# Streaming encoder, two layers: a shared pool of PSUM banks, a later place for layer 1's constants, other places for the norm sums

## The chip, the cores and the metric

One core of a Trainium2 chip runs the whole program. The metric is the device time of one execution in microseconds (us), the median of three runs. The engines are TensorE (PE; its weight loads are PEld), VectorE (DVE), ScalarE (ACT) and GpSimd (POOL); SyncE (SP) issues the transfers.

## What is computed

A two-layer encoder for 512 frames of one new stream and 16 frames of each of 8 running streams, all in fp32, model width 1024. Each layer is

```
h    = rmsnorm(x) @ w_in            # u_a, g_a, u_b, q, k, v
a    = rglru(conv4(u_a)) * gelu(g_a)             # gated linear recurrence, 256 wide
b    = s5(u_b); z = gelu(b + d*u_b); b = z*sigmoid(z @ w_glu)   # complex diagonal recurrence
c    = attention(rope(q), rope(k), v)            # 8 query heads, 2 kv heads, chunks of 64,
                                                 # window 128, one sink per head
x    = x + concat(a, b, c) @ w_out
x    = x + square(relu(rmsnorm(x) @ w_up)) @ w_down           # 1024 -> 4096 -> 1024
```

and one rmsnorm stands at the end. Outputs are y for both kinds of stream and the new states (convolution tail, recurrence states, rotated keys and values).

## The kernel before

Columns are frames, rows are features. The frames are split into two groups `g` of 320 (256 of the new stream, 64 of four running streams), kept in `xT` for the whole run. A product of 128 output rows and 320 frames is a `Unit`: its weights (two halves of 4 tiles) are loaded by SP, split by ACT (`wh`, L243) and DVE (`wl`, L244) into two fp32r parts, and multiplied in three passes (L274 to L276), 12 matmuls for each half of the contraction, 24 for a unit and a group. The very first projection (layer 0, group 0) is done in plain fp32 instead, 4 matmuls a half (L271; the profile shows two rows for each).

`stream(items)` (L278) turns a list of units and plain calls into a generator that yields after each half. A unit takes one of three "mm" banks of PSUM; its evacuation is called in the middle of the next unit, by `clear()` (L285), and put off as long as the unit's norm has no factor `r` yet. `Norm` (L332) squares the rows as they come, `flush()` sums them by ones-matmuls (L374), `finish()` takes the reciprocal root on DVE (L387 to L401) and spreads it by three matmuls (L411) and an ACT copy (L413), with high priority.

Three mixers run beside the projections and the MLP: `lru` (gates L759), `s5` (transposes L176, input products L822, scan L837 to L845, output products L855 and L858, gate L886) and `attention` (`own` L916, `sprobs` L948, `probs` L983, `turned` L999, `sturned` L957, `values` L1012, `svalues` L965; softmax in `soft`, L924 to L946). They are generators too; `TURNS` (L1055) writes their order by hand, `weave` (L322) mixes their steps with halves of the surrounding stream.

PE executes in the written order (L1158). On the other engines a planner orders the instructions when the kernel is built: by its own estimate of when each is ready, the earlier in the program first, high priority ahead of all. A pool slot (a bank, a buffer) is given to a tile when an earlier one is released.

PSUM has eight banks, split by tag: 3 "mm", 2 "att" (attention, the gates of lru, the turn of v in group 0), 2 "s5", 1 "fin" (norm sums). `sprobs` and `probs` take two banks each and hold them until the last exponential (L936) has read them. `own` takes one, released by the copy L922.

`layer_small` (L614) and `s5_const` (L528) prepare a layer's small matrices: four complex products (`cmul`, L545 to L548; for layer 1 all on POOL), transposes of the result (L553), four more products for C (L561 to L564), the product M (L570), then the tables of cosine and sine by doubling (L584 to L605). They use the one table `tab`, which layer 0's s5 reads until its last scan. For layer 1 they are called at the last MLP chunk of layer 0's first group (L1210 to L1213).

The MLP runs in four chunks of 8 `up` and 8 `down` units (`mlp`, L1102), chunks 1 and 2 with both groups per unit. `up_evac` (L1095) is DVE L1097, ACT L1098, POOL copy L156 (called in L1099), DVE L1100; its tile `t` has two buffers.

Of the kernel before, what the change touches and what calls it, by code (L numbers as in the profile page):

```python
# [19 lines left out]
NG = 320  # L20
# [127 lines left out]
def encoder_kernel(ctx: ExitStack, tc: tile.TileContext, a, o):  # L148
# [16 lines left out]
    pm = pool("pm", 1, space=bass.MemoryType.PSUM)  # L165
    banks = {"mm": 3, "att": 2, "s5": 2, "fin": 1}

# [89 lines left out]
    class Unit:  # L257


        def __init__(self, src, prods, norm=None, full=False, raws=None):  # L260
            self.src, self.prods, self.norm, self.full, self.raws = src, prods, norm, full, raws
            self.w = None

# [14 lines left out]
    def stream(items):  # L278


        items = list(items)
        units = [i for i in items if isinstance(i, Unit)]
        wait, late = [], []

        def clear(all_=False):  # L285
            for f in late:
                f()
            late.clear()
            while wait and (wait[0][0].norm is None or wait[0][0].norm.r is not None):
                unit, evac, pt = wait.pop(0)  # L290
                more = evac(pt)
                if more is not None:
                    late.append(more)

        for it in items:
            if not isinstance(it, Unit):
                it()
                continue
            it.load()
            n = units.index(it) + 1  # L300
            if n < len(units):
                units[n].load()
            for m, evac in it.prods:
                m = m() if callable(m) else m
                pt = bank("mm")[:, 0:NG]
                for half in range(2):
                    it.half(pt, m, half)
                    if half == 0:
                        clear()
                    yield  # L310
                wait.append((it, evac, pt))
            it.w = None
        clear()
        clear()
        assert not wait
# [212 lines left out]
    def s5_const(L, K):  # L528
# [21 lines left out]
        for q in range(2):  # L550
            b = bank3("s5", 4, 128)
            for i in range(4):
                transpose(b[:, i], Rp[:, 4 * q + i].rearrange("p r s c -> p (r s c)"))  # L553
            act(K["B"][:, 4 * q:4 * q + 4], b, AF.Copy)
# [12 lines left out]
        yield  # L567
        b = bank("s5")[:, 0:256].rearrange("p (k r c) -> p k r c", k=8, r=2)
        for k in range(8):
# [76 lines left out]
    def in_evac(L, P, g, q, kind, i, pt):  # L646
# [17 lines left out]
        elif kind == "ub":  # L664
            tt(q.ub[:, i], pt, r, OP.mult)
        elif kind == "ga":
            t = tp.tile([128, NG], F32, tag="t", name="t", bufs=2)
            tt(t, pt, r, OP.mult)
            gelu2(V, q.ga[:, i], t)
        elif kind == "v":  # L670
            vT = tp.tile([128, NG], F32, tag="t", name="t", bufs=2)
            tt(vT, pt, r, OP.mult)
            gcopy(q.vS, vT[:, 256:320])

            def turn():
                b = bank3("mm" if g else "att", 2, 128)
                for j in range(2):
                    transpose(b[:, j], vT[:, 128 * j:128 * j + 128])
                act(kvs[L]["vt"][:, 2 * g:2 * g + 2], b, AF.Copy)
                dma(o["vs"][L, g], q.vS)  # L680
                if g == 1:
                    dma(o["vp"][L], kvs[L]["vt"][:, 3])

            return turn
        else:
            sw = tp.tile([128, NG], F32, tag="sw", name="sw", bufs=2)
            for p in range(0, 128, 64):
                act(sw[p:p + 32], pt[p + 32:p + 64], AF.Copy)
                act(sw[p + 32:p + 64], pt[p:p + 32], AF.Copy)  # L689
            G.tensor_tensor(sw, sw, q.sinr, OP.mult)  # L690
            if kind == "q":
                t = tp.tile([128, NG], F32, tag="t", name="t", bufs=2)
                tt(t, pt, q.cosr, OP.mult)
                tt(q.q[:, i], t[:, 0:256], sw[:, 0:256], OP.add)
                v4 = lambda z: z[:, 256:320].rearrange("p (b t) -> p b t", t=16)
                tt(q.qS[:, :, i], v4(t), v4(sw), OP.add)
            else:
                t = tp.tile([128, NG], F32, tag="t", name="t", bufs=2)
                tt(t, pt, q.cosr, OP.mult)  # L699
# [8 lines left out]
    def in_proj(L, g, norm, q, raws=None):  # L708
# [11 lines left out]
        def factors():  # L720
# [5 lines left out]
            for t in (q.cosr, q.sinr):  # L726
                G.tensor_tensor(t, t, q.r, OP.mult)

        evac = lambda kind, i: lambda pt: in_evac(L, None, g, q, kind, i, pt)
        items = [Unit(w_in[n], [(lambda: norm.h, evac(kind, i))], norm, norm.full, raws if n == 0 else None)  # L730
                 for n, (kind, i) in enumerate(units)]
        return [begin, items[0], norm.flush, items[1], factors] + items[2:]


    def lru(L, P, g, q, mix, c):
# [15 lines left out]
        for ct in range(2):  # L751
# [5 lines left out]
            for n, dst in enumerate((t_, i_)):  # L757
                b = bank("att")[:, 0:LP]
                mm(b, lhsT=P["bd"][n][:, ct], rhs=xc, start=True, stop=True)  # L759
# [31 lines left out]
    def s5(L, P, g, q, mix, c):  # L791
# [9 lines left out]
        for ct, gs in cts:  # L801
            if ct:
                yield
            u2 = c.at(640 * ct, 8, 4, 16, parts=80)
            b = bank3("s5", 4, 128)[0:80]
            for t in range(4):
                transpose(b[:, t], u[:, ct, t::4])
            act(u2.rearrange("p g t c -> p t g c"), b.rearrange("p t (g c) -> p t g c", c=16), AF.Copy)
        for ct, gs in cts:
            yield  # L810
            u2 = c.at(640 * ct, 4, 128, parts=80)
            b = bank3("s5", 4, 80)
            for k in range(4):
                transpose(b[:, k], u2[:, k])
            V.tensor_copy(Us[:, ct], b)
        for ct, gs in cts:
            yield
            d, jz = D[:, gs], J[:, gs]
            bs = [bank3("s5", 4, 80) for r in range(2)]
            for k in range(4):  # L820
# [26 lines left out]
        for ct, gs in cts:  # L847
            yield
            d = D[:, gs]
            y2 = c.at(1280 + 640 * ct, 4, 4, 32, parts=80)  # L850
            bs = [bank3("s5", 4, 64)[0:80] for r in range(2)]
            tc2 = lambda t: t.rearrange("p t c -> p (t c)")
# [8 lines left out]
        for ct, gs in cts:  # L861
            y2 = c.at(1280 + 640 * ct, 4, 4, 32, parts=80)
            yield
            b = bank3("s5", 4, 80)
            for t in range(4):
# [17 lines left out]
        for ct in range(2):  # L883
            b = bank("s5")[:, 0:NG]
            for k in range(2):
# [10 lines left out]
    def attention(L, P, g, q, mix, c, cs):  # L896
# [19 lines left out]
        def own():  # L916
            b = bank3("att", 4, 128)[0:16]
            for hf in range(2):
# [29 lines left out]
        def sprobs():  # L948
            bs = [bank3("att", 2, 256) for hf in range(2)]
            for hf, b in enumerate(bs):  # L950
# [6 lines left out]
        def sturned(hf):  # L957
            b = bank3("att", 4, 128)
            for n in range(2):
# [5 lines left out]
        def svalues(hf):  # L965
            b = bank3("att", 2, 64)
            for n in range(2):
# [15 lines left out]
        def probs(cq):  # L983
# [3 lines left out]
            if cq < 2:  # L987
                for pe in pes:
                    G.memset(pe[:, :, 0:64], 0.0)
                    G.memset(pe[:, :, 256:320], 0.0)  # L990
            bs = [bank3("att", 2, 256) for kv in range(2)]
            for pr in range(2):
# [6 lines left out]
        def turned(cq, kv):  # L999
            j, kts, nk, k0, st, w0 = geo(cq)  # L1000
            b = bank("att").rearrange("p (t n q) -> p t n q", t=2, n=2)
            for kt in kts:
# [9 lines left out]
        def values(cq):  # L1012
            j, kts, nk, k0, st, w0 = geo(cq)
            b = bank("att")[:, 0:256]
            for kv in range(2):
# [72 lines left out]
    def out_proj(L, g, mix, hm):  # L1088
# [4 lines left out]
        return [begin] + [Unit(a["w_out"][L, k], [(lambda: mix["mix"](0), evac(k))]) for k in range(8)]  # L1093

    def up_evac(norm, am, f, pt):  # L1095
        t = tp.tile([128, NG], F32, tag="t", name="t", bufs=2)
        V.scalar_tensor_tensor(t, pt, 0.0, norm.r, OP.max, OP.mult)  # L1097
        act(t, t, AF.Square)  # L1098
        gcopy(am[:, f, 0], t)  # L1099
        tt(am[:, f, 1], t, am[:, f, 0].bitcast(F32), OP.subtract)  # L1100

    def mlp(L, c, gs, hm, nxt=None, norms=None, fresh=()):  # L1102
# [17 lines left out]

        ups = [Unit(a["w_up"][L, 8 * c + f], [up(g, f) for g in gs], hm[gs[0]] if fresh and f < 2 else None) for f in range(8)]
        items = [begin] + ups + [Unit(a["w_down"][L, c, k], [down(g, k) for g in gs]) for k in range(8)]
        for g in fresh:
            items[2:2] = [lambda g=g: hm[g].flush()]
            items[4:4] = [lambda g=g: hm[g].finish()]
        return items
# [53 lines left out]
    for L in range(DEPTH):  # L1180
# [15 lines left out]
        run(stream(mlp(L, 0, (1,), hm, fresh=(1,))))  # L1196
        run(stream(mlp(L, 1, (0, 1), hm)))
        run(stream(mlp(L, 2, (0, 1), hm)))
        nxt = (lambda g: Norm(g, None)) if last else (lambda g: Norm(g, n1(L + 1)))
        norms = {}  # L1200
        F = stream(mlp(L, 3, (0,), hm, nxt, norms))
        if last:
            run(F)
            end = [norms[0].flush, lambda: finals(0)]
            items = mlp(L, 3, (1,), hm, nxt, norms)
            items[3:3] = end[:1]
            items[5:5] = end[1:]
            run(stream(items))
        else:
            P = {}  # L1210
            small = layer_small(L + 1, P)
            next(small)
            weave(small, 2, F, 24)  # L1213
            run(F)
# [36 lines left out]
```

## Time and profile before

| | |
|---|---|
| median of 3 runs | 1453.31 us (1453.0 to 1453.5) |
| the profiled execution | 1452.91 us, of which its span in the trace 1451.1 |
| TensorE | 1374.8 us busy (95%), mean granted clock 0.968 |
| VectorE, ScalarE, POOL | 882.4 (61%), 651.5 (45%), 360.0 us (25%) |
| DMA | 156.24 MB, mean 108 GB/s |

In a timeline a row is: start and duration in us, engine, line, operation, output tile <- input tiles, shape, count; in brackets the idle time of the engine ahead of it and what ended it. In the waits, "A <- B: total, times, longest" is idle time of A that B's end ended. "PEclk" is the granted TensorE clock as a share of full speed. Times of a matmul row overlap with the next row's.

### The profile page before, as it was taken

To read this page: it belongs to the slowest core of one execution; us is meant where nothing else is said; L and a number is where in the kernel's file an instruction comes from. 1 tells how busy PE (TensorE), PEld (TensorE's weight loads), DVE (VectorE), ACT (ScalarE), POOL (GpSimd) and SP (SyncE) were. 2 spreads that over 40 slices of the span, in tenths; PEclk is the share of its full clock that TensorE was granted. 3 is DMA by queue.
4 is the path that set the end of the run, shared out by engine and by line. 5 is a ranking of instruction groups with operands and counts; after the bars stand their busy time and mean duration, and the time that the engine had idled before them with its cause. 6 is when DMAs were issued, how large, how long until landed. Compare 5 with 4: busy or idle time off the path is not lost.

```text
span 1451.1 us, 25432 instructions
## 1 busy us (share of the span) xinstructions
PE 1374.8 (95%) x9444; PEld 1313.1 (90%) x9444; DVE 882.4 (61%) x1726; ACT 651.5 (45%) x1347; POOL 360.0 (25%) x581
## 2 busy tenths in 40 slices
PE   7867979999999999999989998899999999999997
PEld 5656869899999999999978998899999999999997
DVE  7785698756644344357787768775664434434674
ACT  4354765545433123134675668553543312313543
POOL 5654277601001001008343224320100100100111
PEclk9978989999999999999999999999999999999998
DMA  6211332344422222233423342333443222223452
GB/s 244 83 55 50 107 104 86 105 154 141 151 95 75 79 79 75 73 110 119 155 90 104 123 128 82 112 96 130 146 145 102 73 73 78 76 80 104 152 175 94
DMA packets 91387, 156.24 MB, mean 108 GB/s; under 512 B 14336, under 2 KB 18304, under 8 KB 91264
## 3 DMA queue, kind: packets, MB, share of 16 engines
q1 hardware_dynamic: 91264, 154.63, 31.9%
q8 instruction: 74, 1.21, 0.3%
q14 instruction: 49, 0.40, 0.1%
HBM read 151.02 MB, written 3.37 MB: 106 GB/s over the span
## 4 chain that ended last, share of the span: by engine, by line
PE 84%; DVE 7%; POOL 3%; ACT 2%; issue 2%; DMA 2%; SPq 0%; DVEq 0%; ACTq 0%; POOLq 0%
PE mm L274 26%; PE mm L275 25%; PE mm L276 25%; PE att L176 1%; PE att L1017 1%; PE s L858 1%; PE att L996 1%; PE fin L411 1%; PE s L886 1%; PE att L971 1%; PE s L822 1%; DVE wl L244 1%; DMA raw<-w_in 1%; PE s L176 0%; PE fin L374 0%
## 5 line engine op out<-in xcount | busy, mean ns | idle before, releaser
L274 PE MATMUL mm<-bigr,wh 128*128 128x320 f32 x2592 | 820.1, 316 | 1.6 <-POOL bigr L156 1.6
L276 PE MATMUL mm<-bigr,wl 128*128 128x320 f32 x2592 | 806.1, 311 | 1.1 <-DVE wl L244 1.1
L275 PE MATMUL mm<-bigr,wh 128*128 128x320 f32 x2592 | 806.5, 311 | 0.3 <-DVE bigr L1100 0.3
L243 ACT ACTIVATE wh<-raw 128x512 fp32r<-128x512 f32 x520 | 327.4, 631 | 508.5 <-PE mm L275 479.4
L274 PEld LDWEIGHTS mm<-bigr,wh 128*128 128x128 f32 x2592 | 492.1, 190 | 15.5 <-issue 8.8
L275 PEld LDWEIGHTS mm<-bigr,wh 128*128 128x128 f32 x2592 | 492.5, 190 | 1.5 <-DVE bigr L1100 0.6
L276 PEld LDWEIGHTS mm<-bigr,wl 128*128 128x128 f32 x2592 | 491.9, 190 | 1.4 <-DVE wl L244 1.4
L244 DVE TENSOR_TENSOR wl<-raw,wh 128x512 fp32r<-128x512 f32 x520 | 377.0, 726 | 190.1 <-ACT wh L243 179.7
L156 POOL TENSOR_SCALAR bigr<-t 128x320 fp32r<-128x320 f32 x128 | 61.0, 478 | 648.5 <-ACT t L1098 648.5
L1084 DVE TENSOR_TENSOR xT<-xT,mm 128x320 f32<-128x320 f32 x160 | 77.7, 486 | 130.4 <-PE mm L276 130.3
L1097 DVE SCALAR_TENSOR_TENSOR t<-mm,r 128x320 f32<-128x320 f32 x128 | 62.3, 489 | 87.9 <-PE mm L276 87.3
L1098 ACT ACTIVATE t<-t 128x320 f32<-128x320 f32 x128 | 60.1, 472 | 114.0 <-DVE t L1097 107.9
L1100 DVE TENSOR_TENSOR bigr<-t,bigr 128x320 fp32r<-128x320 f32 x128 | 65.4, 511 | 68.9 <-POOL bigr L156 68.7
L368 POOL TENSOR_TENSOR ss<-ss,sq 128x320 f32<-128x320 f32 x58 | 55.1, 950 | 185.3 <-ACT sq L361 180.9
L361 ACT ACTIVATE sq<-xT 128x320 f32<-128x320 f32 x66 | 30.5, 462 | 21.5 <-POOL ss L368 14.1
L348 ACT ACTIVATE bigr<-xT,sm 128x320 fp32r<-128x320 f32 x56 | 30.6, 560 | 14.7 <-DVE xT L1084 13.6
L690 POOL TENSOR_TENSOR sw<-sw,cs 128x320 f32<-128x320 f32 x20 | 17.9, 897 | 68.2 <-ACT sw L689 54.4
L996 PE MATMUL att<-kT,q 64*64 64x192 f32 (+2 forms) x256 | 16.6, 347 | 19.1 <-ACT att L936 19.1
L271 PE MATMUL mm<-bigf,raw 128*128 128x320 f32 x104 | 32.2, 456 | 2.5 <-DVE t L699 2.5
L349 DVE SCALAR_TENSOR_TENSOR bigr<-xT,sm,bigr 128x320 fp32r<-128x320 f32 x56 | 34.0, 611 | 0.7 <-ACT bigr L348 0.4
L996 PEld LDWEIGHTS att<-kT,q 64*64 64x64 f32 x256 | 9.4, 147 | 24.1 <-ACT att L936 21.3
L271 PEld LDWEIGHTS mm<-bigf,raw 128*128 128x128 f32 x104 | 20.3, 201 | 10.9 <-DVE t L699 3.0
(297 smaller groups left out, 1107.8 us busy)
## 6 DMA issues: line engine op xcount, KB each, us to landing
raw<-w_up SPq DMA_DIRECT2D x192, 256.0 KB, 2.6
raw<-w_down SPq DMA_DIRECT2D x192, 256.0 KB, 2.6
raw<-w_in SPq DMA_DIRECT2D x85, 256.0 KB, 2.7
raw<-w_out SPq DMA_DIRECT2D x64, 256.0 KB, 2.6
wl<-w_in SPq DMA_DIRECT2D x11, 256.0 KB, 2.8
xT<-x SPq DMA_DIRECT2D x8, 320.0 KB, 5.8
yT<-xT SPq DMA_DIRECT2D x8, 320.0 KB, 2.9
cs<-rope SPq DMA_DIRECT2D x4, 320.0 KB, 2.8
```

Of the source, the lines that this page charges most:

```text
L156: return G.tensor_scalar(out, in_, 1.0, 0.0, OP.mult, OP.add)
L243: act(h, raw, AF.Copy)
L244: tt(l, raw, h.bitcast(F32), OP.subtract)
L271: mm(pt, lhsT=self.w[n][:, k % 4], rhs=m[:, k], start=k == 0, stop=k == 7)
L274: mm(pt, lhsT=h[:, k % 4], rhs=m[:, k, 0], start=k == 0, stop=False)
L275: mm(pt, lhsT=h[:, k % 4], rhs=m[:, k, 1], start=False, stop=False)
L276: mm(pt, lhsT=l[:, k % 4], rhs=m[:, k, 0], start=False, stop=k == 7)
L368: G.tensor_tensor(self.ss, self.ss, sq, OP.add)
L1084: tt(xT[:, g, k], xT[:, g, k], pt, OP.add)
L1097: V.scalar_tensor_tensor(t, pt, 0.0, norm.r, OP.max, OP.mult)
L1098: act(t, t, AF.Square)
L1100: tt(am[:, f, 1], t, am[:, f, 0].bitcast(F32), OP.subtract)
```

## The change

One pool "sm" of four banks takes the place of "att" and "s5"; v's turn uses it in both groups. A unit may carry a call `mid`, made between its first half and `clear()`; the norm's flush and finish, which were items between units, become `mid` of units 1 and 2, in the input projection and in the first MLP chunk; at the end, group 0's flush becomes `mid` of the second up unit of the last chunk and `finals(0)` that of the fourth. The evacuations of the plain fp32 projection are put in high priority. The first part of `layer_small(1)` is traced after 16 halves of the second MLP chunk (chunk 1), its POOL and DVE instructions tied in issue order behind the last up evacuation traced by then; the rest is woven into the third chunk (chunk 2), one step ahead of its first half, one after 20 halves.

```diff
-    banks = {"mm": 3, "att": 2, "s5": 2, "fin": 1}
+    banks = {"mm": 3, "sm": 4, "fin": 1}
...
-            self.w = None
+            self.w = self.mid = None
...
                     if half == 0:
+                        if it.mid:
+                            it.mid()
+                            it.mid = None
                         clear()
...
-                b = bank3("mm" if g else "att", 2, 128)
+                b = bank3("sm", 2, 128)
...
-        evac = lambda kind, i: lambda pt: in_evac(L, None, g, q, kind, i, pt)
+        def evac(kind, i):
+            def f(pt):
+                with tc.high_priority() if norm.full else ExitStack():
+                    return in_evac(L, None, g, q, kind, i, pt)
+
+            return f
...
-        return [begin, items[0], norm.flush, items[1], factors] + items[2:]
+        items[1].mid, items[2].mid = norm.flush, factors
+        return [begin] + items
...
+    mark = {}
+
     def up_evac(norm, am, f, pt):
...
-        gcopy(am[:, f, 0], t)
-        tt(am[:, f, 1], t, am[:, f, 0].bitcast(F32), OP.subtract)
+        mark["pool"] = gcopy(am[:, f, 0], t)
+        mark["dve"] = tt(am[:, f, 1], t, am[:, f, 0].bitcast(F32), OP.subtract)
...
-        ups = [Unit(a["w_up"][L, 8 * c + f], [up(g, f) for g in gs], hm[gs[0]] if fresh and f < 2 else None) for f in range(8)]
+        ups = [Unit(a["w_up"][L, 8 * c + f], [up(g, f) for g in gs], hm[gs[0]] if fresh and f < 3 else None) for f in range(8)]
...
-            items[2:2] = [lambda g=g: hm[g].flush()]
-            items[4:4] = [lambda g=g: hm[g].finish()]
+            ups[1].mid, ups[2].mid = (lambda g=g: hm[g].flush()), (lambda g=g: hm[g].finish())
...
-        run(stream(mlp(L, 1, (0, 1), hm)))
-        run(stream(mlp(L, 2, (0, 1), hm)))
+        F = stream(mlp(L, 1, (0, 1), hm))
+        weave(iter(()), 1, F, 16)
+        if not last:
+            P = {}
+            small = layer_small(L + 1, P)
+            with tc.issue_after(mark["pool"].ins), tc.issue_after(mark["dve"].ins):
+                next(small)
+        run(F)
+        F = stream(mlp(L, 2, (0, 1), hm))
+        if not last:
+            weave(small, 2, F, 40)
+        run(F)
...
-            end = [norms[0].flush, lambda: finals(0)]
             items = mlp(L, 3, (1,), hm, nxt, norms)
-            items[3:3] = end[:1]
-            items[5:5] = end[1:]
+            items[2].mid, items[4].mid = norms[0].flush, lambda: finals(0)
...
-            P = {}
-            small = layer_small(L + 1, P)
-            next(small)
-            weave(small, 2, F, 24)
```

Every other `bank("att")`, `bank3("att", ...)`, `bank("s5")` and `bank3("s5", ...)` becomes "sm", with nothing else changed.

## Rows read from the trace of the kernel before

**Rows 1.** The page, part 1: busy us (share of span) and instructions of each engine.

```profile
PE 1374.8 (95%) x9444; PEld 1313.1 (90%) x9444; DVE 882.4 (61%) x1726; ACT 651.5 (45%) x1347; POOL 360.0 (25%) x581
```

**Rows 2.** Windows: length, busy us (instructions) of PE, PEld, DVE, ACT, POOL; PEclk, DMA, GB/s.

```profile
80.00:125.00 45.00, 26.98 (x145) 22.41 (x146) 32.43 (x61) 23.26 (x58) 22.36 (x35) 0.66 0.10 34
...
195.00:226.00 31.00, 21.98 (x127) 19.66 (x126) 26.99 (x40) 18.15 (x40) 26.36 (x38) 0.72 0.25 81
...
1002.00:1440.00 438.00, 437.50 (x2987) 437.04 (x2985) 222.44 (x395) 160.75 (x279) 41.59 (x74) 1.00 0.32 109
```

**Rows 3.** Waits of PE: us in total, times, longest.

```profile
PE att L996 <- ACT att L936: 19.1, 6, 5.9
...
PE att L953 <- issue: 10.3, 3, 5.5
...
PE s L822 <- DVE bigf L829: 4.4, 7, 1.3
...
PE att L1017 <- ACT bigf L936: 3.8, 3, 2.4
```

**Rows 4.** Timeline of PE, first projection: start, us, instruction, count, idle before.

```profile
16.02 1.41 PE L374 MATMUL fin<-ones,ss 128*128 128x1 f32 x6 [4.06 <-DVE bigf L436]
...
50.20 2.42 PE L271 MATMUL mm<-bigf,raw 128*128 128x320 f32 x8 [2.51 <-DVE t L699]
...
55.37 0.69 PE L176 MATMUL att<-ident,t 128*128 128x128 f32 x2 [2.75 <-DVE t L672]
...
61.49 1.04 PE L176 MATMUL s<-ident,tab 128*128 128x128 f32 x8
```

**Rows 5.** Timeline of DVE, same stretch: the last product of L522.

```profile
55.71 0.42 DVE L522 TENSOR_TENSOR tab<-tab 128x256 f32<-128x256 f32 x1
```

**Rows 6.** Timelines of PE, DVE and POOL, layer 0, second group.

```profile
202.88 1.23 PE L953 MATMUL att<-att,qS 64*64 64x144 f32 x8 [3.15 <-issue]
...
225.35 0.60 PE L176 MATMUL att<-ident,att 128*128 128x128 f32 x4
...
201.95 0.83 DVE L922 COPY att<-att 16x256 f32<-16x256 f32 x2
...
222.01 1.27 POOL L946 TENSOR_SCALAR att<-att,st 128x144 f32<-128x144 f32 x2
```

**Rows 7.** Windows of L274 alone, ahead of 225.35: length, PE, PEclk, DMA, GB/s.

```profile
218.00:225.40 7.40, 4.76 (x12) 0.70 0.14 42
```

**Rows 8.** Timelines of PE and POOL, layer 1, first and second group.

```profile
760.72 1.22 PE L953 MATMUL att<-att,qS 64*64 64x144 f32 x8 [5.53 <-issue]
...
776.08 0.60 PE L176 MATMUL att<-ident,att 128*128 128x128 f32 x4
...
772.38 1.27 POOL L946 TENSOR_SCALAR att<-att,st 128x144 f32<-128x144 f32 x2
...
901.57 0.71 PE L953 MATMUL att<-att,qS 64*64 64x144 f32 x8 [1.58 <-issue]
...
919.45 0.60 PE L176 MATMUL att<-ident,att 128*128 128x128 f32 x4
...
915.38 1.27 POOL L946 TENSOR_SCALAR att<-att,st 128x144 f32<-128x144 f32 x2
```

**Rows 9.** Timelines of PE and DVE, first MLP chunk of layer 0's first group.

```profile
253.92 0.97 PE L411 MATMUL fin<-ident,rsq 128*128 128x128 f32 x6
...
255.39 0.89 DVE L1097 SCALAR_TENSOR_TENSOR t<-mm,r 128x320 f32<-128x320 f32 x2
```

**Rows 10.** The page's groups L276 and L244, PE at 668, DVE beside POOL's tables.

```profile
L276 PE MATMUL mm<-bigr,wl 128*128 128x320 f32 x2592 | 806.1, 311 | 1.1 <-DVE wl L244 1.1
...
L244 DVE TENSOR_TENSOR wl<-raw,wh 128x512 fp32r<-128x512 f32 x520 | 377.0, 726 | 190.1 <-ACT wh L243 179.7
...
668.19 0.41 PE L274 MATMUL mm<-bigr,wh 128*128 128x320 f32 x1 [1.62 <-POOL bigr L156]
...
680.94 1.54 DVE L244 TENSOR_TENSOR wl<-raw,wh 128x512 fp32r<-128x512 f32 x1
```

More of the change, by code (lines that the diff above doesn't have):

```diff
@@ L550, in s5_const @@
         for q in range(2):
-            b = bank3("s5", 4, 128)
+            b = bank3("sm", 4, 128)
             for i in range(4):
@@ L567, in s5_const @@
         yield
-        b = bank("s5")[:, 0:256].rearrange("p (k r c) -> p k r c", k=8, r=2)
+        b = bank("sm")[:, 0:256].rearrange("p (k r c) -> p k r c", k=8, r=2)
         for k in range(8):
@@ L757, in lru @@
             for n, dst in enumerate((t_, i_)):
-                b = bank("att")[:, 0:LP]
+                b = bank("sm")[:, 0:LP]
                 mm(b, lhsT=P["bd"][n][:, ct], rhs=xc, start=True, stop=True)
@@ L804, in s5 @@
             u2 = c.at(640 * ct, 8, 4, 16, parts=80)
-            b = bank3("s5", 4, 128)[0:80]
+            b = bank3("sm", 4, 128)[0:80]
             for t in range(4):
@@ L811, in s5 @@
             u2 = c.at(640 * ct, 4, 128, parts=80)
-            b = bank3("s5", 4, 80)
+            b = bank3("sm", 4, 80)
             for k in range(4):
@@ L818, in s5 @@
             d, jz = D[:, gs], J[:, gs]
-            bs = [bank3("s5", 4, 80) for r in range(2)]
+            bs = [bank3("sm", 4, 80) for r in range(2)]
             for k in range(4):
@@ L850, in s5 @@
             y2 = c.at(1280 + 640 * ct, 4, 4, 32, parts=80)
-            bs = [bank3("s5", 4, 64)[0:80] for r in range(2)]
+            bs = [bank3("sm", 4, 64)[0:80] for r in range(2)]
             tc2 = lambda t: t.rearrange("p t c -> p (t c)")
@@ L863, in s5 @@
             yield
-            b = bank3("s5", 4, 80)
+            b = bank3("sm", 4, 80)
             for t in range(4):
@@ L883, in s5 @@
         for ct in range(2):
-            b = bank("s5")[:, 0:NG]
+            b = bank("sm")[:, 0:NG]
             for k in range(2):
@@ L916, in own @@
         def own():
-            b = bank3("att", 4, 128)[0:16]
+            b = bank3("sm", 4, 128)[0:16]
             for hf in range(2):
@@ L948, in sprobs @@
         def sprobs():
-            bs = [bank3("att", 2, 256) for hf in range(2)]
+            bs = [bank3("sm", 2, 256) for hf in range(2)]
             for hf, b in enumerate(bs):
@@ L957, in sturned @@
         def sturned(hf):
-            b = bank3("att", 4, 128)
+            b = bank3("sm", 4, 128)
             for n in range(2):
@@ L965, in svalues @@
         def svalues(hf):
-            b = bank3("att", 2, 64)
+            b = bank3("sm", 2, 64)
             for n in range(2):
@@ L990, in probs @@
                     G.memset(pe[:, :, 256:320], 0.0)
-            bs = [bank3("att", 2, 256) for kv in range(2)]
+            bs = [bank3("sm", 2, 256) for kv in range(2)]
             for pr in range(2):
@@ L1000, in turned @@
             j, kts, nk, k0, st, w0 = geo(cq)
-            b = bank("att").rearrange("p (t n q) -> p t n q", t=2, n=2)
+            b = bank("sm").rearrange("p (t n q) -> p t n q", t=2, n=2)
             for kt in kts:
@@ L1013, in values @@
             j, kts, nk, k0, st, w0 = geo(cq)
-            b = bank("att")[:, 0:256]
+            b = bank("sm")[:, 0:256]
             for kv in range(2):
```

## The prediction

> **What bounds the kernel now.** I read the page first, then TensorE's idle time stretch by stretch, then what ended each idle gap. TensorE is busy 95% of the span [rows 1], so only its gaps and its slow stretches can be gained. Its fixed price is seen where nothing disturbs it: 438 us for 2987 matmuls at a granted clock of 1.00, 0.147 us each [rows 2]. The gaps lie where the mixers run beside the projections: 45 us at the first attention hold 18.0 us of idle time at a mean clock of 0.66, and 31 us in layer 0's second group hold 9.0 us at 0.72 [rows 2]; layer 1 has two more such places. Low clock comes there after a gap: the 7.4 us ahead of 225.35, at 0.70, hold 12 matmuls of each of the three kinds [rows 7], and 36 x 0.147 is 5.3. I use that loss, 2 us, as the price of one long gap.
>
> The waits name the cause [rows 3]. The largest, 19.1 us, is probs (L996) waiting for ScalarE's exponentials (L936), which is no need of data: probs reads q and kT. Both "att" banks still hold sprobs' scores until the exponentials have read them. The second, 10.3 us put down to "issue", is sprobs' own second bank: its matmuls at 202.88 start 0.1 us after own()'s copy L922 (201.95 + 0.83) [rows 6]. values (L1017) waits 3.8 us for the same banks, and S5's second pair (L822) 4.4 us for L829.
>
> **The change part by part.**
>
> *Four shared banks.* What they remove is a wait for space; what is late next is sturned(0), which needs the normalised probabilities, so it can't move ahead of L946. From the end of sprobs' matmuls to the end of POOL's L946 the chain of maximum, exponentials, sum and scaling takes 223.28 - 204.11 = 19.2 us in layer 0's second group [rows 6], 773.65 - 761.94 = 11.7 and 916.65 - 902.28 = 14.4 in layer 1's two [rows 8]. VectorE is nearly full in those stretches (26.99 of 31 us [rows 2]), so I leave the chain its length, except in layer 0's second group: there POOL is busy 26.36 of 31 us, the constants that the change moves away among its work, and the nearest row without them is the same step of layer 1, 14.4; it gains 4.8.
> sprobs itself ends earlier by the wait at its second half, plus the second-pair waits of L822, taken as 0.5 to 1.1 each (4.4 us over seven waits). So the probabilities come earlier by 3.15 + 1.1 + 4.8 = 9.0, 5.53 + 0.5 = 6.0 and 1.58 + 1.1 = 2.7 us. TensorE reached sturned(0) 2.1, 2.4 and 2.8 us after them (225.35, 776.08, 919.45 [rows 6, 8]); that slack goes too, since all its waits ahead of that point are gone. Gains: 11.1, 8.4 and 5.5. TensorE will now stand before sturned(0) instead, so each keeps one long gap at 2 us: 9.1 + 6.4 + 3.5 = 19.0. For the first attention of layer 0 I take 2.5, under the least of the three, as its stretch has the most idle time but all engines take part in it. Together 21.5. From below: if the chain ends when it ends now, only the slack 2.1 + 2.4 + 2.8 and the 4.8 are left, 12.1, less 8 for four gaps: 4. From above: every chain at 11.7, so 2.7 more in two places, 0.5 in the first, and no gap long enough to cost clock: 35.5.
> values' 3.8 us: the second branch's two banks are often free then; half, 1.9 (0 to 3.8). The v turn leaves the "mm" banks of group 1, where no row shows a wait for them: 0.
>
> *Evacuations of the first projection first (high priority).* TensorE waits 2.51 us for k's product L699 and 2.75 us for v's L672, both queued on VectorE among layer 0's constants [rows 4]. Moving the norm sums into the middle of unit 1 lets half a unit, 2.42 us (8 matmuls, the row at 50.20), run in the 4.06 us gap. That is 7.7, but the next matmul that needs a constant is the transposes at 61.49, and their last input L522 ends at 56.13 [rows 4, 5]: it hangs on VectorE's queue, so evacuations put ahead of it push it. TensorE can come forward by 61.49 - 56.13 = 5.4 at most, less the two q evacuations that go ahead (about 1.1 each), 3.2, less part of a gap's clock: 2. Bounds -4.5 (four q evacuations ahead of the tables, all paid at L815's wait) to 7.7.
>
> *Norm sums and factors half a unit later elsewhere.* Unit 0's bank must be free when unit 2 ends. The broadcast ends at 254.89 and the two L1097 at 256.28, the first about 0.45 before [rows 9]: 0.95 us, hidden by the half unit that still follows it, 12 x 0.147 = 1.76. Nothing; without that cover, up to 0.95 at each of four fresh norms.
>
> *Layer 1's constants behind the second MLP chunk.* Removed from the mixers: the first four complex products, 6 + 6 + 6 + 3 = 21 POOL instructions (L545 to L548). They share the stretch with the one wait of TensorE on L244, 1.1 us [rows 10]; I drop it, 1. Added: those 21 between up evacuations of chunk 1, then the transposes and the tables in chunk 2. SP issues the same transfers, gg and twice bc and six of Mm, among weight loads at a DMA share of 0.32 [rows 2]: free; without cover, a weight tile or two late, 5 us. Evacuation copies on POOL queue behind constants; in the last chunk of layer 0 this cost 1.62 us [rows 10] and some clock. Two groups per unit in chunk 2 give each copy one product more, 24 x 0.147 = 3.5 us, so I take that wait as gone and keep 1 (-2 to 3).
> L244, two SBUF inputs, takes 1.54 us beside POOL's tables against 0.73 on average [rows 10]. The Trainium skill (SBUF — State Buffer, Who interferes with whom) says that such a VectorE instruction and a reading POOL instruction exclude each other for a whole instruction. The trace agrees in kind; the rule speaks against putting tables beside evacuations: by it L1100 could end a POOL instruction later, and the 1 us above would be nothing. The time would then be 1 us higher.
>
> *The finals of group 0* move by half a unit either way, and no row shows a wait of TensorE for them, and the whole second group's last chunk still follows. Nothing.
>
> **Sum.** 21.5 + 1.9 + 2 + 1 + 1 = 27.4 us. The profiled execution took 1452.91 (span 1451.1, 1.81 around it): 1425.5. The median of the runs, 1453.31, is 0.40 above it: 1426.
>
> **Rivals.**
> A. *The wait only changes places* (chance 0.24): VectorE takes maxima and scalings when it does now, whatever TensorE does. For: its fullness. Against: L930 follows sprobs in the program and is ahead of the fill's weights. 4 + 1.9 + 2 + 1 + 1 = 9.9: 1443.
> B. *The softmax follows TensorE* (0.13): 35.5 + 3.8 + 2 + 1 + 1 = 43.3: 1410. For: 11.7 happens with VectorE full. Against: the exponentials still queue behind the gates on ScalarE.
> C. *One branch holds the other's banks* (0.08), slower. sprobs and probs(0) together hold all four, later probs and a turn do; S5's five steps after its scan (four mixers, twenty steps) used to have two of their own. A wait for a bank costs 19.1 / 6 = 3.2 us [rows 3]. Nine of the twenty eat the 27.4; at fourteen the time is 1426 + 14 x 3.2 = 1471. Against: in the written order two attention steps and fill lie between S5 steps, time for the exponentials to release.
> D. *The planner undoes it* (0.06): nothing on the other engines is pinned but the constants' first part; the same waits return elsewhere, 1450 to 1456.
>
> **How the numbers follow.** My case has 0.49 (1413 to 1437). A measurement of this kernel tells about 0.2%, 2.9 us. Faster: my case, A's part below 1450 and B, 0.86; same 0.06 (D and A's edge); slower 0.08 (C). The range reaches from B with half of the start's further room, 1410 - 3 = 1407, to A with the start's lower bound, -4.5 for 2, 1443 + 6.5 = 1450; outside lie C, most of D and B's far end.
>
> **What would show it.** Right: no wait of L996 or L953 for L936 or L922; the longest wait at the transposes of sturned(0); no L520 to L526 of layer 1 on POOL between 200 and 240 us; the waits at 50 and 55 us gone. Wrong: sturned(0) starts in all four places within 2 us of where it starts now, counted from the start of that mixer; new waits at S5's L855 or L176 for L936; or a new wait at 85 us longer than the present one.

## The result, and the profile after

The changed kernel takes **1427.72 us** (median of four executions, 1423.95 to 1429.21) against 1453.32 in the same rounds: a ratio of 0.982, with a 95% interval of 0.980 to 0.984. The forecast was 1426 in 1407 to 1450. The profiled execution took 1423.95 us, its span is 1422.1, and TensorE's mean granted clock rose from 0.968 to 0.981. Lines of the code have moved by 3 to 12: L996, L953, L946, L930 and L936 of before are L1006, L963, L956, L940 and L946 now, and the "att" and "s" tiles of PSUM are "sm".

The page, part 1, answers to [rows 1]: the same 9444 matmuls, 16 us less of busy time and, by the span, 13 us less of idle time.

```profile
PE 1358.9 (96%) x9444; PEld 1300.3 (91%) x9444; DVE 876.0 (62%) x1726; ACT 651.7 (46%) x1347; POOL 359.4 (25%) x581
```

The windows of the first attention and of layer 0's second group [rows 2]. TensorE works 31.78 instead of 26.98 us of the first, and its clock in the second is 0.89 instead of 0.72. VectorE is busy 28.67 of 31 us in the second: fuller than before.

```profile
80.00:125.00 45.00, 31.78 (x262) 27.20 (x264) 32.86 (x69) 27.96 (x76) 24.11 (x43) 0.77 0.14 48
185.00:216.00 31.00, 22.79 (x150) 20.24 (x146) 28.67 (x54) 22.61 (x54) 18.36 (x30) 0.89 0.33 106
```

The waits of TensorE, to be held against [rows 3]. The four waits for banks are gone. Two others have come in their stead: 19.1 us at the transposes of sturned (L176) for VectorE's scaling L956, and 12.7 us of the projections' matmuls for the split of the weights, L244, which had cost 1.1.

```profile
PE sm L176 <- DVE att L956: 19.1, 4, 10.4
PE mm L276 <- DVE wl L244: 12.7, 5, 4.1
PE sm L832 <- DVE bigf L825: 6.2, 1, 6.2
```

To see where the time went, I compared when each of the 2592 matmuls of L276 runs, in its order, in the profiled executions (before minus the other kernel), and cut the run where the mixers of a group begin or end. "Whole" is the gain at the last one. These are single executions; the change itself stands there twice, and shows how far a stage can differ. Both times its profiled execution was the fastest of its four.

```
gain in us by stage     to first  first      layer 0  MLP, layer  layer 1  layer 1  whole  median
                        fill      attention  group 1  1's input   group 0  group 1         of runs
the change              11.2      2.3        6.1      2.8         4.8      1.8      29.0   1427.7
the change, again       10.0      3.3        4.6      2.8         4.9      1.8      27.4   1428.6
banks alone              7.3      1.5       -1.6     -0.1         4.8      1.7      13.7   1439.4
constants alone         -0.1      0.0        3.3      2.8         0.5      0.1       6.5   1445.6
change, old constants    9.9      0.2       -2.0      0.1         4.9      0.8      14.0   1437.3
change, old banks        3.6      1.5        1.0      2.8        -1.9      0.4       7.3   1445.7
change, old norm sums    6.2      1.4        8.2      2.8         4.9      0.5      23.9   1428.2
three empty steps in 3  10.8      1.3        7.6      2.8         4.9      2.9      30.1   1421.6
```

(Group 0's first attention in layer 0 ends with the second column, where group 1's mixers begin. Behind the sixth column no kernel gains or loses more than 0.1.)

The sum was right and its parts were not. The first group's way to the end of its first attention gave 13.5 us where the prediction had about 5; the three later attentions gave 12.7 where it had 19.0, and most of values' 1.9 on top.

### The profile page after: what moved, and what is told of

It reads as the page before. It is cut to its first block, busy times and chain, and to the rows that moved or that the text cites. A ratio compares the mean times of both kernels' runs of the same rounds, so it can differ in the third digit from the quotient of the medians.

```text
span 1422.1 us, 25428 instructions
## 1 busy us (share of the span) xinstructions
PE 1358.9 (96%) x9444; PEld 1300.3 (91%) x9444; DVE 876.0 (62%) x1726; ACT 651.7 (46%) x1347; POOL 359.4 (25%) x581
## 4 chain that ended last, share of the span: by engine, by line
PE 82%; DVE 9%; POOL 4%; issue 2%; ACT 1%; DMA 0%; SPq 0%; DVEq 0%; ACTq 0%
PE mm L274 25%; PE mm L275 25%; PE mm L276 25%; PE sm L176 2%; DVE wl L244 1%; PE mm L271 1%; PE sm L1027 1%; DVE bigf L853 1%; DVE bigf L850 1%; PE sm L868 1%; PE fin L414 1%; PE sm L981 1%; PE sm L896 1%; PE sm L1006 1%; PE sm L832 0%
## 5 line engine op out<-in xcount | busy, mean ns | idle before, releaser
L274 PE MATMUL mm<-bigr,wh 128*128 128x320 f32 x2592 | 817.6, 315 | 2.1 <-POOL bigr L156 1.8
L276 PE MATMUL mm<-bigr,wl 128*128 128x320 f32 x2592 | 805.3, 311 | 12.7 <-DVE wl L244 12.7
L274 PEld LDWEIGHTS mm<-bigr,wh 128*128 128x128 f32 x2592 | 490.2, 189 | 15.7 <-issue 5.8
L276 PEld LDWEIGHTS mm<-bigr,wl 128*128 128x128 f32 x2592 | 490.4, 189 | 14.0 <-DVE wl L244 14.0
L244 DVE TENSOR_TENSOR wl<-raw,wh 128x512 fp32r<-128x512 f32 x520 | 375.9, 724 | 181.2 <-ACT wh L243 169.5
L1112 DVE TENSOR_TENSOR bigr<-t,bigr 128x320 fp32r<-128x320 f32 x128 | 71.0, 556 | 71.5 <-POOL bigr L156 71.2
L176 PE MATMUL sm<-ident,att 128*128 128x128 f32 x88 | 13.9, 289 | 19.7 <-DVE att L956 19.1
L956 POOL TENSOR_SCALAR att<-att,st 128x192 f32<-128x192 f32 (+2 forms) x24 | 22.6, 950 | 39.5 <-ACT wh L243 31.0
L352 DVE SCALAR_TENSOR_TENSOR bigr<-xT,sm,bigr 128x320 fp32r<-128x320 f32 x56 | 30.4, 551 | 0.1
```

Source lines behind the costliest of these rows:

```text
L244: tt(l, raw, h.bitcast(F32), OP.subtract)
L274: mm(pt, lhsT=h[:, k % 4], rhs=m[:, k, 0], start=k == 0, stop=False)
L276: mm(pt, lhsT=l[:, k % 4], rhs=m[:, k, 0], start=False, stop=k == 7)
L1112: mark["dve"] = tt(am[:, f, 1], t, am[:, f, 0].bitcast(F32), OP.subtract)
```

## The experiments

**One part alone, and all but one.** The edits: for the banks alone, on the kernel before:

```
-    banks = {"mm": 3, "att": 2, "s5": 2, "fin": 1}
+    banks = {"mm": 3, "sm": 4, "fin": 1}
```

with every "att", "s5" and the v turn's "mm" made "sm"; the same undone on the kernel after for the old banks; `in_evac` called without the high priority; norm.flush, factors, the MLP's flush and finish and the finals back between the units; and layer 1's constants (`layer_small`, its two marks and the weave) put back into the last chunk, or moved alone on the kernel before.

The banks alone:

> The kernel before with the four shared banks alone. Theory 1 (the banks carry the change, as the prediction has it: 21.5 + 1.9 of 27.4): 1430 to 1436. Theory 2 (what the trace after shows gained by the end of the first attention's start, 11 us, is owed to the early evacuations, and the banks give only the steps at layer 0's second group and layer 1's first, some 5 + 4): 1441 to 1446. If constants in the old place fill VectorE and POOL at layer 0's second group, that step is under 5 us here.

1439.43 us, ratio 0.991 (0.9894 to 0.9927). Between the theories, and the last sentence came true: layer 0's second group lost 1.6 us. The waits of TensorE and, in that group, the first maximum and POOL's own part of the scaling:

```profile
PE sm L176 <- DVE att L946: 20.3, 4, 10.6
PE mm L276 <- DVE wl L244: 12.9, 5, 4.1
...
PE sm L176 <- POOL att L946: 2.8, 2, 2.1
```

```profile
188.69 1.20 PE L953 MATMUL sm<-att,qS 64*64 64x144 f32 x16
...
198.28 0.44 DVE L930 TENSOR_REDUCE st<-sm 128x2 f32<-128x288 f32 x1
...
207.41 1.17 POOL L520 TENSOR_TENSOR tab<-s5s,tab 128x256 f32<-128x256 f32 x1
...
211.32 1.14 POOL L522 TENSOR_TENSOR tab<-tab 128x256 f32<-128x256 f32 x1
...
214.76 1.27 POOL L946 TENSOR_SCALAR att<-att,st 128x144 f32<-128x144 f32 x2
```

From the end of sprobs' matmuls to the end of POOL's scaling it is 216.03 - 189.89 = 26.1 us, against 19.2 before: the scores come earlier, the maximum does not follow them, and POOL's scaling stands behind the constants' products.

The change with the old banks:

> The kernel after with the two att and two s5 banks put back, all else of the change kept. Theory 1: 1446 to 1452, and the waits of probs for the exponentials (19 us before) and of sprobs' second bank (10 us) are back. Theory 2: 1436 to 1442. If early evacuations need the banks to keep what they gain, the first transposes of B come 5 us earlier here too, but the gain is gone by the end of the first attention.

1445.65, ratio 0.9949 (0.9934 to 0.9964): nearer theory 1. The waits for the exponentials (17.2) and for sprobs' second bank (11.8) are back, and the 5 us by which the first transposes of B come earlier here too end as 3.6 at the first fill.

The change without the high priority:

> The kernel after without the high priority of the first projection's evacuations. Theory 1 (they are worth the 2 us of the prediction or the 5 us that the trace has at the transposes of B, no more): 1430 to 1433. Theory 2 (they carry the 11 us of the start, since a shorter gap there also keeps the granted clock up): 1437 to 1440.

1428.64 (1423.14 to 1429.27), no difference from the change, under the bounds of both theories. In this trace the transposes of B start at 57.32 against 56.57 with it: that is what it moves, 0.75 us of the 4.9.

The change with the old constants:

> The kernel after with layer 1's constants back in the last MLP chunk of group 0 and in layer 0's second mixer. Theory 1 (prediction: 1 + 1, and 4.8 of the banks' gain at layer 0's second group hangs on POOL being free of constants): 1432 to 1436. Rival (the new place costs as much in waits for the weights' L244, 3.6 + 4.1 + 2.7 us, as it frees): 1426 to 1430.

1437.25, ratio 0.9893 (0.9878 to 0.9908): the move is worth 9.5 us when the banks are shared, more than theory 1 had. By stage, 6.6 to 8.1 of it lie in layer 0's second group (4.6 or 6.1 against -2.0).

The change with the norm sums in their old places:

> The kernel after with the norm sums, the factors and the finals back in their old places, between units. Theory 1 (the prediction's 0 elsewhere and a part of the 2 at the start): 1428 to 1431. Theory 2 (the run without high priority is as fast as the kernel after and still 3 us ahead of the run with the banks alone at the first transposes and the first fill, so the later norm sums are what gains at the start): 1431 to 1434, with 2 us lost before the first fill and the wait of L377 at 16 us back at 4 us.

1428.20 (1427.94 to 1428.96): in time theory 1, no difference. Its trace has what theory 2 named, 3.6 us of wait at L377 and a first fill 5.0 us later than in the change, but layer 0's second group gives some of it back, and its profiled execution is, at 1428.96, the slowest of its four, those of the change are their fastest. What the late sums are worth in an ordinary execution is thus under what these medians tell apart.

The constants alone:

> The kernel before with layer 1's constants moved, alone. Theory 1 (the move is worth the 9.5 us that undoing it costs only where the shared banks let the scores out early; alone the old waits for space stand in its way): 1448 to 1453. Rival (POOL and VectorE freed in layer 0's second group are worth the same with either banks): 1441 to 1445.

1445.60, ratio 0.9955 (0.9941 to 0.997): between the two again, 5.9 us against 9.5 beside shared banks. Here the chain of layer 0's second group became what the prediction had taken for the whole change:

```profile
203.03 1.23 PE L953 MATMUL att<-att,qS 64*64 64x144 f32 x8 [3.13 <-issue]
...
217.59 1.29 POOL L946 TENSOR_SCALAR att<-att,st 128x144 f32<-128x144 f32 x2
```

218.88 - 204.26 = 14.6 us, predicted 14.4. So the step that this chain is long because of the constants is right; that it stays so short once the scores come earlier is not.

**Who stands ahead of the softmax.** Two kernels tried to put single instructions first, on the kernel after:

```
         def sprobs():
...
-            soft([b[:, :, 0:144] for b in bs], p, ...)
+            with tc.high_priority():
+                soft([b[:, :, 0:144] for b in bs], p, ...)
```

> The kernel after with the softmax behind sprobs (maximum, exponentials, sum, scaling) issued in high priority, so that its few small instructions no longer stand behind scans, products and weights on VectorE nor behind the square root on ScalarE. Theory 1 (in the four attention starts the chain from the scores to the scaled probabilities sets the end, and what makes it long is its place in the queues): the waits at the first transposes (10.4 + 3.5 + 1.0 + 4.2 us) fall by half or more, 1418 to 1424. Rival (VectorE is full there, and what is put behind is needed just as soon): the wait goes over to the weights' L244 and to S5's steps, 1426 to 1431.

1425.12 (1422.72 to 1425.42), ratio 0.9812 (0.9798 to 0.9827). Its instructions stand in the same order on every engine as in the kernel after: the priority moved none of them, so it tested nothing and is a second timing of the change. It is 3 us from the first and from the third, and that is the size under which I call nothing a difference.

> The kernel after with the two instructions that split a weight tile (ScalarE L243, VectorE L244) in high priority. Theory 1 (12.7 us of TensorE's waits are for L244 behind mixer work on VectorE; the split is needed first, the mixer work later): 1420 to 1425. Rival (VectorE is full: the softmax is late by as much as the weights are early): 1426 to 1432.

1427.57 (1426.87 to 1430.92). Here VectorE's order did change, and L244's wait stayed at 12.7 us while other waits came and went: as the rival has it.

**More work for TensorE before it asks for the probabilities.** If the softmax chain runs on VectorE's time, TensorE's own order can wait for it:

```
-    TURNS = "ALSSLSSSS" "LAAAAAA" + 5 * "SAA" + "A"
+    TURNS = "ALSSLSSSS" "LAAA---AAA" + 5 * "SAA" + "A"
...
-            next(G3[t], None)
+            if t != "-":
+                next(G3[t], None)
```

and three steps more in the weaves of 23, 7 and 15.

> The kernel after with three empty steps in the mixers' order between the first scores of the cache-free attention and the first transposes of the cached one, so that TensorE has 1.5, 2.1, 3.9 and 2.1 more halves of a projection unit (12 matmuls x 0.147 = 1.76 us each) to do before it asks for the probabilities; the fill that is spread over the later steps is less by as much. Theory 1 (with shared banks the softmax chain keeps its length, and what is left of it is only TensorE standing in its own order): 2.7 + 3.5 + 1.0 + 3.6, some 11 us at most, and 6 to 11 come through: 1417 to 1422. Rival (VectorE is full there: the fill's own evacuations, or the later steps that have less fill, put the same wait elsewhere): 1425 to 1430.

1424.46 (1422.74 to 1425.90): between the theories, within what separates two timings of the change. By stage it gained 4.3 and 7.6 in layer 0's two attentions where the change had 2.3 and 6.1, and lost in layer 1's first group, 1.8 for 4.8: there an up evacuation of the MLP fill came late.

```profile
PE mm L276 <- DVE wl L244: 12.7, 9, 4.1
PE sm L176 <- DVE att L956: 9.2, 1, 9.2
...
PE mm L274 <- DVE t L1110: 4.3, 1, 4.3
```

> The same with six empty steps: 2.7, 3.3, 6.0 and 3.3 more halves. Theory 1: the first attention gains 4.8 us instead of 2.7, the others no more than with three, since their waits were covered: 2 us under the run with three, 1415 to 1420. Rival: with so little fill left, waits appear at the later transposes and values, and it is slower than the run with three.

1432.68 (1432.13 to 1433.35): the rival. The later steps lack the fill: L414's broadcast waits 11.1 us in two places, 9.5 in one, and the cached values (L981) and the scores (L1006) together 13.

The last two runs, timed in the same rounds: the change again, and three empty steps in three of the four mixers (`TURNS.replace("-", "")` where (L, g) is (1, 0), and the weave of 15 as before).

> The kernel after, unchanged, beside the run that follows: its times so far lie 5 us apart, so the two are timed in the same rounds. 1424 to 1429.

1428.64 (1425.56 to 1428.69).

> Three empty steps ahead of the first transposes in both groups of layer 0 and in layer 1's second, none in layer 1's first, where they turned a gain of 4.4 us into 1.5 (the MLP fill's own evacuation came 4.3 us late). Theory 1 (the four mixers add up, each with the order that suits it): some 3 us under the run with three everywhere, 1420 to 1423, and 3 to 6 us under the kernel after. Rival (VectorE is full in the mixers, and any order of TensorE's work only places the same idle time): within 2 us of the kernel after.

(That 4.4 and 1.5 are of a stage with other bounds; in the columns above it is 4.8 and 1.8.)

**1421.60** (1420.04 to 1422.30), ratio to the kernel before 0.9785 (0.9772 to 0.9798) against 0.9831 (0.9817 to 0.9844) of the change beside it: 7 us less, and all five executions lie under the least of the twelve of the change (1422.72). The median gap is larger than the 3 to 6 expected, and more than its trace shows (30.1 us of gain for the change's 29.0 and 27.4), so the size is uncertain by about 3 us; that it is the fastest of these kernels is not. Its profiled execution is the slowest of its five, at a mean clock of 0.979; the others had 0.982 to 0.984.

```profile
PE sm L176 <- DVE att L956: 9.6, 1, 9.6
```

Of the four waits of L176 for VectorE's scaling one is left, that of the first attention; in the second group of either layer TensorE now has fill there. In the first attention the same order gained 4.3 us in the run before and 1.3 here, so a stage of a single trace tells no more than some 3 us.

## Why the prediction was right, and which of its steps were not

**The banks were the cause of the old waits: right.** All four kinds of waits in [rows 3] go with the banks and come back with them. Sprobs ends earlier, by somewhat more than the sum of waits said. In the three later starts its end moved from 204.11, 761.94 and 902.28 [rows 6, 8] to 185.17, 732.39 and 870.11, by 18.9, 29.6 and 32.2 us, of which 13.5, 22.4 and 27.2 had been gained when that group's mixers began: 5.4, 7.2 and 5.0 are its own (predicted 3.15 + 1.1, 5.53 + 0.5 and 1.58 + 1.1).

**"I leave the chain its length": wrong, and with it the three later starts.** From the end of sprobs to the end of POOL's scaling it is 21.5, 17.2 and 21.1 us now, where the sum had 14.4, 11.7 and 14.4. The timelines of the kernel after, sprobs, the first maximum, POOL's scaling and the transposes, in layer 0's second group and layer 1's two:

```profile
183.97 1.20 PE L963 MATMUL sm<-att,qS 64*64 64x144 f32 x16
...
193.34 0.45 DVE L940 TENSOR_REDUCE st<-sm 128x2 f32<-128x288 f32 x1
...
204.68 1.96 POOL L956 TENSOR_SCALAR att<-att,st 128x144 f32<-128x144 f32 x2 [0.60 <-ACT sq L364]
...
205.43 0.78 PE L176 MATMUL sm<-ident,att 128*128 128x128 f32 x4 [3.45 <-DVE att L956]
...
731.19 1.20 PE L963 MATMUL sm<-att,qS 64*64 64x144 f32 x16
...
740.65 0.45 DVE L940 TENSOR_REDUCE st<-sm 128x2 f32<-128x288 f32 x1
...
747.95 1.60 POOL L956 TENSOR_SCALAR att<-att,st 128x144 f32<-128x144 f32 x2
...
748.25 0.86 PE L176 MATMUL sm<-ident,att 128*128 128x128 f32 x4 [1.03 <-DVE att L956]
...
868.91 1.20 PE L963 MATMUL sm<-att,qS 64*64 64x144 f32 x16
...
878.75 0.45 DVE L940 TENSOR_REDUCE st<-sm 128x2 f32<-128x288 f32 x1
...
889.28 1.92 POOL L956 TENSOR_SCALAR att<-att,st 128x144 f32<-128x144 f32 x2
...
890.03 1.09 PE L176 MATMUL sm<-ident,att 128*128 128x128 f32 x4 [4.23 <-DVE att L956]
```

The maximum starts 8.2, 8.3 and 8.6 us after the scores are there. Before it started 2.8, 2.6 and 3.7 us after them, by these rows of the kernel before:

```profile
206.90 0.45 DVE L930 TENSOR_REDUCE st<-att 128x2 f32<-128x288 f32 x1
...
764.49 0.45 DVE L930 TENSOR_REDUCE st<-att 128x2 f32<-128x288 f32 x1
...
906.00 0.45 DVE L930 TENSOR_REDUCE st<-att 128x2 f32<-128x288 f32 x1
```

So 5 to 6 us of the earliness are eaten before the first instruction of the softmax: counted from where its mixers begin, the maximum starts 0.1, 1.5 and 0.1 us earlier than before. VectorE has other work in its queue, without a break (8.97 us busy of the 9 from 186), and comes to the maximum in its own order. In layer 0's second group it runs the same seven instructions between own()'s copy and the maximum in both kernels, and from the start of the one to that of the other it is 4.95 us before (201.95 [rows 6], 206.90) and 4.91 after (188.43, 193.34). Two of the seven are L244 of the fill's weights, which the prediction, in its argument against rival A, had put behind the maximum:

```profile
188.43 0.83 DVE L932 COPY att<-sm 16x256 f32<-16x256 f32 x2
...
191.28 1.11 DVE L244 TENSOR_TENSOR wl<-raw,wh 128x512 fp32r<-128x512 f32 x1
...
192.71 0.71 DVE L244 TENSOR_TENSOR wl<-raw,wh 128x512 fp32r<-128x512 f32 x1
```

The banks alone show the same: the maximum moves by 206.90 - 198.28 = 8.6 us where 8.8 had been gained.

By the same count the end of the chain moved by 16.6 - 13.5 = 3.1, 24.1 - 22.4 = 1.7 and 25.5 - 27.2 = -1.7 us, where the sum had 9.0, 6.0 and 2.7. This is rival A's mechanism, which had a chance of 0.24: in the three later starts it is what happened, and the waits for L244, which no case foresaw, are its other half. These starts still gave 12.7, since the slack ahead of the transposes (2.1 to 2.8 us) came in, and some more, as the first of them wait for VectorE's part of the scaling and start 1.2 us before POOL's ends: they come 6.4, 5.5 and 2.3 us earlier. TensorE's clock in layer 0's second group, 0.89 instead of 0.72, came in too. The run with three empty steps in three mixers agrees: TensorE's order gives way, and in the second groups of both layers the transposes find their data. That it is VectorE's queue which holds the maximum is read from the traces; no run took it forward in that queue, since the priority moved nothing.

What values' bank gave back in layer 0's second group, a wait of 2.35 us before, was lost right behind it to a new wait of the MLP fill for POOL's copy, with 0.53 us more for L1112; what made that copy late is not shown.

```profile
269.20 0.41 PE L274 MATMUL mm<-bigr,wh 128*128 128x320 f32 x1 [1.76 <-POOL bigr L156]
```

**"For the first attention of layer 0 I take 2.5": wrong by some 6 us, the other way.** I took the least of the three others for a stretch whose rows I had not priced. The waits in it, in the kernel before (the gates' tanh L760 holding a bank of own(), the exponentials those of probs):

```profile
100.30 1.01 PE L176 MATMUL att<-ident,vS 128*16 128x128 f32 x4 [2.87 <-ACT bigf L760]
...
111.86 0.47 PE L996 MATMUL att<-kT,q 64*64 64x64 f32 x2 [4.94 <-ACT att L936]
```

with 1.68 us at the second pair of S5's matmuls make 9.5 us. With the banks alone, sprobs' matmuls start at 95.87 instead of 103.77, and at the end of this attention the kernel is 8.8 us ahead. VectorE could follow here: its first maximum in the kernel after starts 2.0 us after the scores (1.4 before), so this chain grew only from 12.3 to 14.9 us. The 10.4 us at L176 came down to 9.2 and 9.6 with the empty steps: three of them are too few there.

**The start: 2 us forecast, 4.9 in the trace at the transposes of B.** TensorE reaches them at 56.57 instead of 61.49 [rows 4], and they wait for VectorE's table L525, as the cap by L522 had said. The cap of 5.4 was nearly reached.

```profile
16.26 0.80 PE L377 MATMUL fin<-ones,ss 128*128 128x1 f32 x6 [2.12 <-DVE bigf L439]
...
46.81 3.96 PE L271 MATMUL mm<-bigf,raw 128*128 128x320 f32 x8 [2.42 <-DVE t L702]
...
56.57 1.09 PE L176 MATMUL sm<-ident,tab 128*128 128x128 f32 x8 [1.27 <-DVE tab L525]
...
81.58 3.71 PE L832 MATMUL sm<-bigf,Bm 64*128 64x80 f32 x32 [6.16 <-DVE bigf L825]
```

With the old norm sums these transposes start at 61.79, without the priority at 57.32: the late sums bring them forward, not the priority, to which the prediction had given the larger part. The gap at 16 us shrank by 1.94. In this trace k's product L702 is waited for as long as before and v's wait is gone; in the second one it is 0.7 us for k and 1.2 for v, so some 2 of their 5.3 us stayed. One step later, at 81.58, 3.5 us are left, and the wait for S5's input has grown from 5.2 to 6.2; the prediction's lower bound had allowed 4.5 more. In the medians neither half of this part, priority or late sums, can be seen when it is taken away.

**The constants: 1 + 1 + 4.8 of the chain forecast, 9.5 measured with shared banks and 5.9 without.** The removed wait at 668 [rows 10] was under-priced: it stood at 1 us for a stall of 1.62 + 0.33, its clock left out. TensorE's windows behind it, in the kernel before:

```profile
664.00:668.00 4.00, 2.56 (x18) 2.30 (x16) 2.03 (x4) 1.16 (x3) 3.92 (x11) 1.00 0.43 144
668.00:672.00 4.00, 3.49 (x14) 3.26 (x15) 3.08 (x4) 1.54 (x3) 3.92 (x9) 0.69 0.16 56
672.00:676.00 4.00, 4.00 (x27) 4.00 (x26) 2.35 (x3) 2.15 (x4) 4.00 (x9) 0.88 0.36 123
```

4 us at 0.69 and 4 at 0.88 lose 1.2 + 0.5 = 1.7; with the two stalls 3.7 us. Against it stands one new wait in the second chunk, of a matmul for L1112 (L1100 of before), with VectorE and POOL beside it:

```profile
563.70 0.42 PE L275 MATMUL mm<-bigr,wh 128*128 128x320 f32 x1 [1.06 <-DVE bigr L1112]
```

```profile
562.12 1.52 DVE L1112 TENSOR_TENSOR bigr<-t,bigr 128x320 fp32r<-128x320 f32 x1 [0.98 <-POOL bigr L156]
```

```profile
562.05 1.24 POOL L604 TENSOR_TENSOR tab<-tab 128x496 f32<-128x496 f32 x1
```

L1112 takes 1.52 us there and 0.56 on average over the run. The Trainium skill (SBUF — State Buffer, Who interferes with whom) says that a VectorE instruction with two SBUF inputs and a POOL instruction that reads exclude each other; the prediction had weighed that this would end L1100 later and cost its 1 us. The trace agrees in kind, but the 1.06 us have a second cause: VectorE had waited 0.98 us for POOL's copy before L1112 could start. What was wrong is the other side: 3.7 us were to be had, and 3.7 - 1.1 = 2.6 is near what the constants alone gained in this stage, 2.8.

The larger part of the 9.5 is in layer 0's second group, where the constants' products stand ahead of the softmax on POOL, as the windows and POOL's rows of the banks alone show. Not all of them have left it. Only the first part of the constants is tied in issue order; the 21 products for C, written into the third chunk, have no such tie, and the planner placed them in layer 0's second group all the same: two ahead of the softmax and 19 in the MLP fill, from 239.56 to 258.96. What these cost no run shows.

```profile
190.71 1.13 POOL L523 TENSOR_TENSOR tab<-s5s,tab 128x256 f32<-128x256 f32 x1 [2.55 <-DVE tab L562]
...
239.56 0.85 POOL L524 TENSOR_TENSOR Cm<-s5s,tab 128x256 f32<-128x256 f32 x1
```

**The finals and the later norm sums: 0 forecast.** Right: behind the sixth column every kernel's gain stays within 0.1 us, with the later sums and without.

**The signs that it had named.** The waits of L996 and L953 are gone, and the longest wait stands at the transposes of sturned(0), as for a right forecast. Of the others, two came only in part: some 2 of the 5.3 us of waits at 50 and 55 us stayed, and one of layer 1's products on POOL falls between 200 and 240. Two signs of a wrong one came in small: S5's output products (L855, now L865) wait 0.6 us in all for the exponentials, and the wait for S5's input at 85 us, now at 82, is 0.9 longer.

**The chances.** The likeliest case gave the time by two errors of some 9 and 8 us that cancelled (13.5 for 4.5 at the first group, 12.7 for 20.9 behind it); that the time was hit so closely is luck. The case that VectorE's fullness decides the starts deserved more than 0.24, as the row for it (26.99 of 31 us busy, [rows 2]) was read and then used for the opposite: here the first instruction of a chain on a full engine kept its *time*, and the chain did not keep its length.

## What to carry to other kernels

When a wait for space is taken away, ask in whose queue the consumer of the freed work stands: on an engine that was busy nine tenths of the stretch it was taken, in this case, when it had been taken before, and little more than TensorE's slack behind it was won. Price every wait of a stretch by its own rows before one takes a figure over from another stretch. Once the wait has moved to the order of TensorE's own work, try a few units of independent work ahead of it, place by place: three empty steps gained at the starts of the two second groups and lost at one of the first, six gained at none.

## What the runs showed of the hardware

A wait of 4.10 us costs TensorE more than itself. In the kernel after, layer 1's first group:

```profile
736.99 0.64 PE L276 MATMUL mm<-bigr,wl 128*128 128x320 f32 x1 [4.10 <-DVE wl L244]
737.42 0.47 PE L274 MATMUL mm<-bigr,wh 128*128 128x320 f32 x1
...
742.75 0.36 PE L276 MATMUL mm<-bigr,wl 128*128 128x320 f32 x1
```

From 737.42 to 742.75 twenty matmuls start 0.267 us apart instead of 0.147, at the lower of the two clock levels, 1.2 GHz (the granted clock from 736 to 740 is 0.50): 2.4 us more, where the prediction had 2 for a long gap. And at 668 a stall of 2 us in all was enough for 1.7 more.

A four-column instruction of VectorE can hold the chain: L942 took 1.49 us in the first attention and 0.22 in the second, the first time beside a product of POOL, with which it ended.

```profile
98.92 1.49 DVE L942 TENSOR_SCALAR st<-st,nsks 128x4 f32<-128x4 f32 x1
...
198.74 0.22 DVE L942 TENSOR_SCALAR st<-st,nsks 128x4 f32<-128x4 f32 x1
```

```profile
98.58 1.81 POOL L854 TENSOR_TENSOR bigf<-bigf,tab 128x640 f32<-128x640 f32 x1 [0.26 <-ACT bigf L852]
```

The Trainium skill (SBUF — State Buffer, Who interferes with whom) names tensor_scalar among the instructions that can block a whole POOL instruction or be blocked by one; these rows agree, 100.41 against 100.39 at the end.

And one program timed three times gave medians of 1427.7, 1425.1 and 1428.6 us, with executions from 1422.7 to 1429.2 us, where the kernel before, in the same sessions, lay between 1450.2 and 1454.1. In each of the three the fastest execution is the one with the highest mean granted clock, 0.981 where the others had 0.978 to 0.979. Why the clock differs is open: only the profiled executions have traces.
